# Hybrid mLSTM and dilated-attention encoder: key parts, query splits, step shares and two row loads placed differently in the second request's part

## The chip, the cores and the metric

The kernel runs on one core of a Trainium2 chip. The metric is the device time of one execution in microseconds (us). The engines are TensorE (PE, matmuls; PEld is its weight load), VectorE (DVE), ScalarE (ACT), GpSimd (POOL) and SyncE (SP, which issues DMA transfers; GpSimd issues some too).

## What is computed

One encoder layer is applied to two requests with the same weights: A (`x_prompt`, 1024 tokens) and B (`x_sample`, 512 tokens), both with 1024 channels.

```
h    = rms_norm(x, pre_w)
cols = h @ w_in                     # q|k, v, o, gates of the mLSTM; q, k, v of the attention; z's; merge gates
y_m  = mlstm_mixer(...)             # 4 heads x 256, forward and backward, chunks of 128
y_a  = dilated_attention(...)       # 3 groups x 8 heads x 64, mixed by their softmax denominators
g    = sigmoid(gate)
out  = (g0 * (y_m @ w_pm) + g1 * (y_a @ w_pa)) @ w_out
y    = x + rms_norm(out, post_w)
```

## The kernel before, in words

**Products.** All large products are float32 split in two parts of fewer bits, high and low: high times high, high times low, low times high. `mm3` (L212, L213, L214) issues these three matmuls; I call them a triple. A weight block arrives by DMA in a raw tile (`load_w`, L264, queue `self.side`), ScalarE writes its high part (L275), VectorE subtracts it for the low part (L281, `split_w`). The same split is made for queries and keys.

**Stages in time.** A's projections come first, up to about 960 us. Then `short_input` (L802) turns B's rows with TensorE transposes (L316) that ScalarE (L322) and VectorE (L323) evict into `H`; a scan of A and A's attention (1310 to 1587 us) follow; then `quad`, B's scan (about 1590 to 1782 us), B's attention (to about 2056 us), B's `combine`, and the remaining products up to the end.

**Fill.** B's projections, and later the output projections, are a list of steps, `Fill`, a step being one triple. They are woven between the instructions of the scans and attentions: `fill.stage(steps, shares)` sets a rate of steps per share, each `fill(share)` brings the count of steps up to what is due by then, and `fill.until(n)` issues what is left up to step n. `quad` asks for its stage with 192 steps (`STEPS`, L2171), of which `fill.until(SHORT)` behind it issues what has not come.

**Order.** TensorE's order is that of the code. ScalarE's, VectorE's, GpSimd's and SyncE's orders in time come from a scheduler that follows its own idea of when inputs are there; `issue_after` adds that an instruction stands behind another. So an edit in one place moves instructions of these engines elsewhere too. Each engine runs its own list strictly in order, and a DMA queue's issues are in such a list.

**quad, B's scan.** Four heads, four chunks of 128 tokens, two directions: 32 rounds. `prepare(h)` splits head h's queries (L1310 on ScalarE, L1311 on VectorE, into tile X1) and, for each chunk c, the keys: kh (L1316) and kl (L1317), one buffer each. Then two triples make the scores sc, and ScalarE evicts them (L1327, `st`). For head 0 it runs as a whole before the rounds, with a fill share of 1/5 between the chunks; for the others it begins in an earlier head's round with i = d = 1, one chunk a round. `front(k)` makes round k's weighted scores: a mask on GpSimd (L1348), an exponential on ScalarE (L1350, `rm`), products on VectorE (L1355, L1356), the high part `sch` on ScalarE (L1363) and the low part `scl` on GpSimd (L1364). `core(k)` multiplies them with the values: `num` (L1377 with sch, L1380 with scl). Its results are divided and accumulated (L1383 to L1389), normalized and, some rounds later, turned (L1407) and stored as `ym_b` (L228 from SyncE). The head's loads are `Q<-qk_b`, `V1a<-vs_b` (SyncE) and `rw<-rw_b` (GpSimd). Fill steps beside it are evicted by L755, L758, L760, L766 (o and z gates, `sw`, `sg`) and L915 (merge gates, stored as `gt_b`).

**B's attention.** `bias<-erow` is loaded by SyncE, the logits lg are made (L1675), VectorE adds the bias and finds the maximum (L1694), ScalarE exponentiates (L1698), TensorE turns the result (L1705). In A's attention the same stages of the 64-wide groups are L1574, L1585, L1589, L1597 and the output's eviction L1612. `attend` ends with `self.held = []` (L1871); until then `held` has its last evictions, behind which weight splits are put.

**combine, B.** For each of four rows: a load of the attention's output (`V0a`, `V1a<-og_b`, 792 KB, L1898) and of a gate (`az_b`, 256 KB, into `az`, `X`, `Q`), weights (L1907 to L1917), a mix (L1924) and sums (L1930) on VectorE, then a turn on TensorE (L1935). The first two rows' loads are issued together from SyncE (L1953 to L1957). Beside it run products with weight blocks `w_out` and `w_pm`, which GpSimd loads (L264). `body` calls `next(mixed)`, sets the last fill stage and issues `fill(4)` (L2409) before it goes on with the rows.

## Time and profile before

| | us |
|---|---|
| median of three runs | 2209.32 (2208.91 to 2210.37) |
| the profiled execution | 2206.59 |
| its span, first to last instruction | 2204.8 |
| TensorE busy in the span | 2185.3 |
| VectorE, ScalarE, GpSimd busy | 1463.5, 1087.3, 696.8 |
| mean granted TensorE clock | 0.998 of full speed |

How to read the profile's rows: a timeline row has start, duration, engine, line, operation and tiles, and in square brackets the idle time ahead of it and what released it. A row of the list of waits has who waited for whom, total us, times, longest. A row of the table by stretches has a stretch of the span, its length, each engine's busy time there with the number of instructions, and the clock that was granted to TensorE (1.00 is full speed). TensorE's rows overlap: a matmul of 512 columns shows some 0.39 us, while the next one starts 0.23 us after it.

### The profile page before, as it was taken

To read this page: it belongs to the slowest core of one execution; us is meant where nothing else is said; L and a number is where in the kernel's file an instruction comes from. 1 tells how busy PE (TensorE), PEld (TensorE's weight loads), DVE (VectorE), ACT (ScalarE), POOL (GpSimd) and SP (SyncE) were. 2 spreads that over 40 slices of the span, in tenths; PEclk is the share of its full clock that TensorE was granted. 3 is DMA by queue.
4 is the path that set the end of the run, shared out by engine and by line. 5 is a ranking of instruction groups with operands and counts; after the bars stand their busy time and mean duration, and the time that the engine had idled before them with its cause. 6 is when DMAs were issued, how large, how long until landed. Compare 5 with 4: busy or idle time off the path is not lost.

```text
span 2204.8 us, 34396 instructions
## 1 busy us (share of the span) xinstructions
PE 2185.3 (99%) x11962; PEld 1886.4 (86%) x11962; DVE 1463.5 (66%) x2969; ACT 1087.3 (49%) x2246; POOL 696.8 (32%) x981
## 2 busy tenths in 40 slices
PE   9999999999999999999999999999999999999998
PEld 8999888888888888888888889998788888888787
DVE  7765665657778555547888765564667855656674
ACT  7322243444444333446777656666655544544332
POOL 1000432333333222226677640011044522232221
PEclk9999999999999999999999999999999999999999
DMA  3842443423233222376746569996778786776763
GB/s 126 194 115 78 156 163 134 172 105 115 106 114 115 80 75 94 134 244 210 229 153 214 152 195 255 247 244 183 227 235 260 232 260 215 228 249 198 249 216 109
DMA packets 209144, 390.41 MB, mean 177 GB/s; under 512 B 37418, under 2 KB 123114, under 8 KB 208971
## 3 DMA queue, kind: packets, MB, share of 16 engines
q1 hardware_dynamic: 179128, 279.63, 40.5%
q0 software_dynamic: 26240, 96.00, 13.6%
q10 hardware_dynamic: 3602, 12.59, 1.4%
q8 instruction: 94, 1.54, 0.3%
q14 instruction: 80, 0.65, 0.1%
HBM read 274.70 MB, written 113.44 MB: 176 GB/s over the span
## 4 chain that ended last, share of the span: by engine, by line
PE 90%; issue 3%; DMA 2%; DVE 2%; POOL 1%; ACT 1%; SPq 0%; DVEq 0%; POOLq 0%; ACTq 0%
PE d L214 14%; PE d L212 14%; PE d L213 14%; PE dense L212 11%; PE dense L213 11%; PE dense L214 11%; PE lg L1675 2%; PE pt L1705 1%; PE o L1748 1%; PE num L212 1%; PE num L214 1%; PE num L213 1%; PE a L1095 1%; DMA wraw<-w_pm 1%; PE kv L212 1%
## 5 line engine op out<-in xcount | busy, mean ns | idle before, releaser
L212 PE MATMUL dense<-H,wh 128*128 128x512 f32 x664 | 269.5, 406 | 0.0
L213 PE MATMUL dense<-H,wh 128*128 128x512 f32 x664 | 260.6, 393 | 0.0
L214 PE MATMUL dense<-H,wl 128*128 128x512 f32 x664 | 260.6, 392 | 0.0
L213 PE MATMUL d<-Hl,phla 128*128 128x512 f32 x608 | 236.5, 389 | 0.0
L214 PE MATMUL d<-Hh,phla 128*128 128x512 f32 x608 | 236.5, 389 | 0.0
L212 PE MATMUL d<-Hh,phla 128*128 128x512 f32 x608 | 236.5, 389 | 0.0
L281 DVE TENSOR_TENSOR wl<-wraw,wh 128x1024 fp32r<-128x1024 f32 (+1 forms) x121 | 149.3, 1235 | 51.5 <-ACT wh L275 51.4
L212 PE MATMUL d<-Hh,phlb 128*128 128x512 f32 x456 | 177.4, 389 | 0.0
L213 PE MATMUL d<-Hl,phlb 128*128 128x512 f32 x456 | 177.4, 389 | 0.0
L214 PE MATMUL d<-Hh,phlb 128*128 128x512 f32 x456 | 177.4, 389 | 0.0
L275 ACT ACTIVATE wh<-wraw 128x1024 fp32r<-128x1024 f32 (+1 forms) x124 | 128.1, 1035 | 61.1 <-PE dense L213 19.5
L214 PEld LDWEIGHTS dense<-H,wl 128*128 128x128 f32 x664 | 124.8, 188 | 28.1
L696 POOL TENSOR_TENSOR psum_w<-pw_raw 128x512 f32<-128x512 f32 x38 | 55.9, 1472 | 280.9 <-DMA pw_raw<-w_in 251.2
L214 PE MATMUL d<-vhi,Hl 128*128 128x322 f32 x448 | 140.5, 314 | 0.5 <-DVE Hl L432 0.3
L212 PE MATMUL d<-vhi,Hh 128*128 128x322 f32 x448 | 140.3, 313 | 0.1
L212 PEld LDWEIGHTS dense<-H,wh 128*128 128x128 f32 x664 | 125.5, 189 | 16.8 <-issue 1.2
L213 PE MATMUL d<-vlo,Hh 128*128 128x322 f32 x448 | 139.6, 312 | 0.0
L1694 DVE CUSTOM_DVE_ANT_0 ls<-lg,bias 128x256 f32<-128x256 f32 (+2 forms) x240 | 78.8, 350 | 90.9 <-PE lg L1675 62.1
L213 PEld LDWEIGHTS dense<-H,wh 128*128 128x128 f32 x664 | 125.6, 189 | 14.9
L212 PEld LDWEIGHTS d<-Hh,phla 128*128 128x128 f32 x608 | 114.2, 188 | 23.6
L213 PEld LDWEIGHTS d<-Hl,phla 128*128 128x128 f32 x608 | 114.2, 188 | 23.6
L214 PEld LDWEIGHTS d<-Hh,phla 128*128 128x128 f32 x608 | 114.2, 188 | 23.6
(630 smaller groups left out, 5809.6 us busy)
## 6 DMA issues: line engine op xcount, KB each, us to landing
pw_raw<-w_in SPq DMA_DIRECT2D x76, 512.0 KB, 4.2
wraw<-w_in SPq DMA_DIRECT2D x63, 512.0 KB, 4.2
aqk_a<-pwk SPq DMA_DIRECT2D x40, 512.0 KB, 3.5
wraw<-w_pm POOLq DMA_DIRECT2D x24, 512.0 KB, 6.1
wraw<-w_out POOLq DMA_DIRECT2D x24, 512.0 KB, 4.1
aqk_b<-sw SPq DMA_DIRECT2D x40, 256.0 KB, 4.7
wraw<-w_v POOLq DMA_DIRECT2D x22, 430.0 KB, 6.8
qk_a<-pwk SPq DMA_DIRECT2D x16, 512.0 KB, 2.7
```

Source lines behind the costliest of these rows:

```text
L212: nc.tensor.matmul(out, lh, rh, start=start, stop=False, **kw)
L213: nc.tensor.matmul(out, lh, rl, start=False, stop=False, **kw)
L214: nc.tensor.matmul(out, ll, rh, start=False, stop=stop, **kw)
L275: high = nc.scalar.activation(hi[:, :n], raw[:, :n], AF.Copy)
L281: low = (self.lows or nc.vector).tensor_sub(lo[:, :n], raw[:, :n], hi[:, :n].bitcast(F32))
L696: self.nc.gpsimd.tensor_add(s[:, 0], ws[1][:, 0], ws[1][:, 1])
L1095: nc.tensor.matmul(p[:, c - c0], kT[:, ct, c * P:(c + 1) * P], qT[:, ct, c * P:(c + 1) * P], start=ct == 0, stop=ct == 1)
L1675: nc.tensor.matmul(lg[:, hh], q[hh][:, qs], z.rearrange("p (n j) -> p n j", j=P)[:, pair], start=z is k[hh], stop=z is not k[hh])
L1694: nc.vector.tensor_tensor_reduce(out=ls[rows, hh], in0=ts["lg"][hh][rows, of], in1=bt[rows, hh, by], scale=1.0, scalar=NEG, op0=OP.add, op ...
L1705: nc.tensor.transpose(pp[:, hh * nk + x], ts["ls"][:, hh, x * P:(x + 1) * P], self.ident)
L1748: nc.tensor.matmul(of(hh, 0, P), vh(kt[x], hh), pt[:, hh * len(kt) + x], start=x == 0, stop=x == len(kt) - 1)
```

## The change

Five edits:

1. `short_input` takes two placeholder banks of the transposes' pool with a memset, where it took one, so that the first transposes begin two banks on.
2. `attend` hands its last evictions on as `self.behind`, and the query split of the scan's head 0 is put behind these; for the other heads it is put behind the newest accumulation.
3. In `prepare`, kh has two buffers and the next chunk's high part is made before the scores of this one; kl, still with one buffer, is made after them. For heads 1 to 3 `prepare` begins a round later (i = 2, d = 0).
4. `quad` asks for 3 shares more for the same 192 steps.
5. In `combine` of B, row 1's two loads go to GpSimd's queue, behind the last weight load and behind one more `yield`; `body` issues `fill(2)`, these loads, `fill(2)`.

```diff
-        nc.vector.memset(ps.tile([P, BLK], F32, name="d")[0:1, 0:1], 0.0)
+        for _ in range(2):
+            nc.vector.memset(ps.tile([P, BLK], F32, name="d")[0:1, 0:1], 0.0)
...
-            fill.stage(steps, lead + len(rounds) + n // 4 + late)
+            fill.stage(steps, lead + len(rounds) + n // 4 + late + 3)
...
-                nc.scalar.activation(qs[0], x["q"], AF.Copy)
-                nc.vector.tensor_sub(qs[1], x["q"], qs[0].bitcast(F32))
-
-                def keys(c):
-                    k = x["k"][:, :, c * P:(c + 1) * P]
-                    kk = [sb.tile([P, 2, P], F32R, name=z, bufs=1) for z in ("kh", "kl")]
-                    nc.scalar.activation(kk[0], k, AF.Copy)
-                    nc.vector.tensor_sub(kk[1], k, kk[0].bitcast(F32))
-                    return kk
-
-                kk = keys(0)
+                of = lambda c: x["k"][:, :, c * P:(c + 1) * P]
+
+                def high(c):
+                    k = sb.tile([P, 2, P], F32R, name="kh")
+                    nc.scalar.activation(k, of(c), AF.Copy)
+                    return k
+
+                def low(c, hi):
+                    k = sb.tile([P, 2, P], F32R, name="kl", bufs=1)
+                    nc.vector.tensor_sub(k, of(c), hi.bitcast(F32))
+                    return hi, k
+
+                with ExitStack() as st_:
+                    for z in self.behind if h == 0 else self.acc[1:]:
+                        st_.enter_context(self.tc.issue_after(z.ins))
+                    nc.scalar.activation(qs[0], x["q"], AF.Copy)
+                    nc.vector.tensor_sub(qs[1], x["q"], qs[0].bitcast(F32))
+                kk = low(0, high(0))
                 yield
                 for c in range(n):
+                    coming = high(c + 1) if c < n - 1 else None
...
-                    kk = keys(c + 1) if c < n - 1 else None
+                    kk = coming is not None and low(c + 1, coming)
...
-                if i == d == 1 and h < 3:
+                if i == 2 and d == 0 and h < 3:
...
-            self.held = []
+            self.behind, self.held = self.held, []
...
-            loads(1)
+            yield
+            with self.tc.issue_after(self.loaded.ins):
+                loads(1, self.side)
...
-                fill(4)
+                fill(2)
+                next(mixed)
+                fill(2)
```

The order on the engines moves with it. First, ScalarE at the start of B's scan, from the second key of head 0 on (names: kh keys' high part, st the scores, wh a weight block's high part, sw and sg gates, sch the first product's scores). Before:

```order
L1316 ACTIVATE kh<-Q_15607 128x256
L1327 ACTIVATE st_15899<-sc 128x512
L1316 ACTIVATE kh<-Q_15607 128x256
L1327 ACTIVATE st_15899<-sc 128x512
L1350 ACTIVATE rm<-rm,col_7710 128x128
L1363 ACTIVATE sch<-rm 128x128
L1327 ACTIVATE st_15899<-sc 128x512
L1350 ACTIVATE rm<-rm,col_7710 128x128
L275 ACTIVATE wh_7698<-wraw_7696 128x1024
L755 ACTIVATE sw_7815<-dense 128x512
L1363 ACTIVATE sch<-rm 128x128
```

In the changed kernel (Q_15609 is head 0's tile, Q_16087 head 1's; L1315 stands for L1316, L1336 for L1327, L1359 for L1350, L1372 for L1363):

```order
L1315 ACTIVATE kh<-Q_15609 128x256 x3
L1336 ACTIVATE st_15901<-sc 128x512
L1315 ACTIVATE kh<-Q_15609 128x256
L1336 ACTIVATE st_15901<-sc 128x512 x3
L1315 ACTIVATE kh<-Q_16087 128x256 x2
L275 ACTIVATE wh_7698<-wraw_7696 128x1024
L755 ACTIVATE sw_7817<-dense 128x512
L1359 ACTIVATE rm<-rm,col_7710 128x128
L766 ACTIVATE sg<-sg,hnw 128x512
L1372 ACTIVATE sch<-rm 128x128
```

The first sch stood ahead of the last score's eviction and of the weight split; now it stands behind head 1's first two keys, the weight split and two gate evictions. VectorE's list has the same move: its part of rm (L1356, now L1365) stood ahead of the low part of that weight block (L281) and of L760 and now stands behind them. On TensorE the first `num` follows the last triple of that weight block directly, where a triple of the next block lay between. SyncE's loads of head 1's queries and keys stood behind a weight load that waits for this split and now stand ahead of it, behind five other loads.

Second, SyncE ahead of B's attention (gt_b stores of gates, ym_b stores of the scan's turns, bias the first tile's bias). Before:

```order
L228 DMA gt_b<-sw_7813 128x512
L228 DMA ym_b<-ym_7822 128x2x128
L228 DMA ym_a<-az_15888 128x4x128
L228 DMA gt_b<-sw_7814 128x512
L228 DMA gt_b<-sw_7815 128x512
L228 DMA ym_b<-ym_7823 128x2x128
L253 DMA bias_18083<-erow 128x256 x2
```

In the changed kernel:

```order
L228 DMA gt_b<-sw_7814 128x512
L228 DMA gt_b<-sw_7815 128x512
L228 DMA ym_b<-ym_7825 128x2x128
L264 DMA wraw_7696<-w_in 128x1024
L253 DMA bias_18083<-erow 128x256 x2
L253 DMA Q_17554<-aqk_b 64x512 x2
L253 DMA V1a<-aqk_b 64x512 x3
L253 DMA Q_17554<-aqk_b 64x512 x2
L253 DMA V1a<-aqk_b 64x512 x3
L253 DMA bias_18084<-erow 128x256 x2
L228 DMA gt_b<-sw_7816 128x512
L228 DMA gt_b<-sw_7817 128x512
```

The stores of the last two gates of this stretch (there sw_7814 and sw_7815, here sw_7816 and sw_7817, the same two tiles) stood ahead of the first bias and now stand behind the second. TensorE's list has 14 dense triples between the last turn (L1407) and the first logits (L1675), where it had none.

Third, GpSimd in B's combine (wraw a weight block's raw tile, X and V1a row 1's loads, xo the residual rows). The change's piece of the list, from the `w_out` block on:

```order
L264 DMA wraw_7697<-w_out 128x1024
L253 DMA ymr_18065<-ym_b 128x512
L264 DMA wraw_7696<-w_pm 128x1024
L253 DMA X_20643<-az_b 128x4x128
L253 DMA V1a<-og_b 128x1584
L2173 DMA xo_20634<-x_prompt 128x512
L2173 DMA xo_20635<-x_prompt 128x512
L264 DMA wraw_7697<-w_pm 128x1024
```

The fourth and fifth row stood on SyncE between `V0a<-og_b` and `Q<-az_b`; all else of this piece is as it was.

More of the change, by code (lines that the diff above doesn't have):

```diff
@@ L1895, in combine, with load @@
         az_of.at = -(T.n - 1) % len(az_of.bufs)
-        def load(t):
-            self.fetch(("og", T.S), cs[t % 2], T.og[t * P:(t + 1) * P])
+        def load(t, queue=None):
+            self.fetch(("og", T.S), cs[t % 2], T.og[t * P:(t + 1) * P], queue)
         by = lambda x: x.rearrange("p g (a b) -> p g a b", a=4)
@@ L1945, in combine, with loads @@
         az, w = {}, []
-        def loads(t):
+        def loads(t, queue=None):
             if t < T.n:
                 az[t] = az_of()
-                self.fetch(("az", T.S), az[t].rearrange("p (c s) -> p c s", c=4), T.az[:, :, t * P:(t + 1) * P].rearrange("c p s -> p c s"))
-                load(t)
+                self.fetch(("az", T.S), az[t].rearrange("p (c s) -> p c s", c=4), T.az[:, :, t * P:(t + 1) * P].rearrange("c p s -> p c s"),
+                           queue)
+                load(t, queue)
         if slow:
```

## The prediction

> **What bounds the kernel now.** I read the page's first part, then the list of TensorE's waits, then the timelines around each wait that the change touches. The page comes first:
>
> ```profile
> PE 2185.3 (99%) x11962; PEld 1886.4 (86%) x11962; DVE 1463.5 (66%) x2969; ACT 1087.3 (49%) x2246; POOL 696.8 (32%) x981
> ```
>
> TensorE is busy for 2185.3 of 2204.8 us, so 19.5 us of idle time is all that an edit which leaves its instructions alone can win, apart from its clock. The change leaves TensorE's products as they are and moves some. So the question is only which waits go, which come, and what the clock does behind them. The waits that the change touches:
>
> ```profile
> PE lg L1675 <- DVE ot L1694: 2.5, 1, 2.5
> PE dense L212 <- ACT Q L275: 1.2, 1, 1.2
> PE sc L214 <- DVE kl L1317: 0.9, 2, 0.6
> PE sc L212 <- ACT kh L1316: 0.9, 2, 0.6
> PE d L316 <- DVE d L802: 0.8, 1, 0.8
> PE dense L213 <- DVE Q L281: 0.8, 1, 0.8
> PE pt L1597 <- ACT ls L1589: 0.7, 2, 0.3
> ```
>
> The columns are total us, times, longest; the seven add up to 7.8 us. Some cost more than they show, as the table by stretches says (stretch, its length, busy time of PE, PEld, DVE, ACT and POOL with instructions in brackets, then the granted clock, DMA share, GB/s):
>
> ```profile
> 1794.40:1797.90 3.50, 3.42 (x12) 3.06 (x13) 1.09 (x8) 3.24 (x10) 0.00 (x0) 0.51 1.04 292
> 2070.90:2074.40 3.50, 3.50 (x10) 2.72 (x10) 3.02 (x6) 0.69 (x2) 2.77 (x6) 0.51 0.92 328
> ```
>
> The first stretch lies right behind the wait of 2.5 us, the second right behind the pair of 1.2 and 0.8. In both the granted clock is 0.51: 3.5 us at half speed lose 3.5 x 0.49 = 1.7 us each.
>
> **Edit 1, the second placeholder (L802).** The memset on a fresh bank waits for the last eviction of the phase before; with two placeholders the first transposes get a bank that was evicted earlier, and VectorE's late eviction is wanted only some transposes later. Gain 0.8 by the waits row, nothing at worst: **-0.8**.
>
> **Edit 2, the query split of the first head.** Here it stands in front of the softmax of attention A:
>
> ```profile
> 1565.90 1.06 ACT L1310 ACTIVATE X<-Q 128x1024 fp32r<-128x1024 f32 x1 [2.22 <-DMA Q<-qk_b]
> 1566.99 1.23 DVE L1311 TENSOR_TENSOR X<-Q,X 128x1024 fp32r<-128x1024 f32 x1 [2.51 <-ACT X L1310]
> ```
>
> ScalarE stands still 2.22 us for the load and then both engines spend 1.06 and 1.23 us, and the transposes of L1597 wait 0.7 us in all. Put behind the last evictions of A, nothing waits for it there: the first scores run at 1597.19 (below). Gain 0 to 1.1 (with what a wait costs beside its mark, see the keys), I take **-0.8**. The splits of heads 1 to 3 move behind the last accumulations of the scan and a round later, and their scores move with them; no wait of TensorE is marked for these splits now, so 0.
>
> **Edit 3, keys.** Start to start a product of 512 columns takes 0.23 us (below, 1606.28 to 1606.50). The first wait of the scan:
>
> ```profile
> 1597.19 0.40 PE L213 MATMUL sc<-X,kh 128*128 128x512 f32 x1
> 1598.19 0.50 PE L214 MATMUL sc<-X,kl 128*128 128x512 f32 x1 [0.60 <-DVE kl L1317]
> ```
>
> It stays, since the low part of key 0 still stands behind a weight split and an eviction on VectorE, and it grows: with a smaller share per step only two filler triples (0.68 us each), not three, come before the first score. **+0.7**. The other three waits (0.9 + 0.9 - 0.6 = 1.2 us) are a head's keys that a single buffer releases late; high parts made a chunk ahead and a preparation that begins a round later take these away. From the first row to the second are 1.00 us, so 0.77 is lost for 0.60 marked; by that ratio 1.2 is worth 1.5: **-1.5**, and 0 if the low part, which still has one buffer, is what comes late.
>
> **What this order costs: the first product of the scan.** ScalarE and VectorE also change their order there. Before, the split of the first scores (rm L1356, sch L1363) was done ahead of the next unit's weight split. Now sch stands behind the high part of head 1's first two keys, L275, L755 and L766, and its input rm behind L281 and L760 on VectorE; L275 itself waits for the unit's last product. And on TensorE the product that needs sch comes directly behind that unit's end, where before one triple lay between. These pieces, in time order, as they run now:
>
> ```profile
> 1606.28 0.39 PE L213 MATMUL dense<-H,wh 128*128 128x512 f32 x1
> 1606.50 0.39 PE L214 MATMUL dense<-H,wl 128*128 128x512 f32 x1
> 1607.20 1.04 ACT L275 ACTIVATE wh<-wraw 128x1024 fp32r<-128x1024 f32 x1
> 1607.32 0.29 DVE L1356 TENSOR_TENSOR rm<-rm,st 128x128 f32<-128x128 f32 x1 [2.50 <-ACT rm L1350]
> 1607.41 0.40 PE L1377 MATMUL num<-V0a,sch 128*128 128x258 f32 x2
> 1608.15 0.58 ACT L755 ACTIVATE sw<-dense 128x512 f32<-128x512 f32 x1
> 1608.27 1.23 DVE L281 TENSOR_TENSOR wl<-wraw,wh 128x1024 fp32r<-128x1024 f32 x1 [0.66 <-ACT wh L275]
> 1608.62 0.30 ACT L1363 ACTIVATE sch<-rm 128x128 fp32r<-128x128 f32 x1
> 1609.77 0.68 DVE L760 SCALAR_TENSOR_TENSOR sg<-sw,sg 128x512 f32<-128x512 f32 x1
> 1610.95 0.71 ACT L766 ACTIVATE sg<-sg,hnw 128x512 f32<-128x512 f32 x1
> ```
>
> On this clock the unit now ends one triple later: its L213 starts at 1606.96 and ends at 1607.35, and TensorE is free at 1607.41. The chain: L275 at 1607.37; L281 1.07 behind it (as 1607.20 to 1608.27) at 1608.44, over at 1609.67; L760 to 1610.3; L766 to 1611.0 (rm is ready meanwhile); sch to 1611.3. The product waits from 1607.4 to 1611.3: **3.9 us**. It is more if the keys ahead of L275 wait for head 1's load, which now goes out early, behind five transfers:
>
> ```profile
> 1591.79 4.74 DMA wraw<-w_in
> V1b<-og_a SPq DMA_DIRECT2D x1, 792.0 KB, 10.3
> Q<-qk_b SPq DMA_DIRECT2D x8, 256.0 KB, 5.2
> ```
>
> Its fourth piece is held until that weight load has landed, at 1596.5; 5.2 us later is 1601.7, 10.3 us later (the slowest transfer of this stretch) is 1606.8. Keys are needed by 1606.6 (two at 0.4 ahead of 1607.4), so 0 to 0.2 more from this, and up to 1 if it queues longer. I take **+4.1**. A wait this long can halve the clock behind it. The two stretches above say 1.7 us for each such window; it falls partly into the wait itself or takes two windows (0 to 3.4): **+1.5**.
>
> **Edit 4, the late products.** The stage's shares go up by 3: 192/38 = 5.05 steps per share becomes 192/41 = 4.68, while 38 shares are drawn, so 192 - 178 = 14 triples are left, 9.5 us of TensorE that now stand ahead of attention B's first logits. What they should cover:
>
> ```profile
> 1780.38 5.40 SPq L228 DMA_DIRECT2D gt_b<-sw  x2
> 1783.88 1.06 ACT L275 ACTIVATE Q<-wraw 128x1024 fp32r<-128x1024 f32 x1 [6.08 <-DMA wraw<-w_in]
> 1786.35 1.00 SPq L253 DMA_DIRECT2D bias<-erow  x2
> 1792.65 0.42 DVE L1694 CUSTOM_DVE_ANT_0 ls<-lg,bias 128x256 f32<-128x256 f32 x1 [5.02 <-DMA bias<-erow]
> 1793.99 0.42 DVE L1694 CUSTOM_DVE_ANT_0 ls<-lg,bias 128x256 f32<-128x256 f32 x1 [0.91 <-DMA bias<-erow]
> 1791.57 0.39 PE L214 MATMUL dense<-H,wl 128*128 128x512 f32 x1
> 1794.48 1.22 PE L1675 MATMUL lg<-V0a,Q 128*128 128x256 f32 x4 [2.52 <-DVE ot L1694]
> ```
>
> SyncE's queue sits 5.40 us on a store whose eviction stands on ScalarE behind a weight split that waits 6.08 us for its load. So the bias goes out at 1786.35, its second half lands at 1793.99, and the logits of the third tile wait: 2.91 from start to start less 0.23 are 2.7 us, and 1.7 of clock behind them. Now the last two gate stores stand behind the bias, which follows the last turn's store at once; 7.6 us (1786.35 to 1793.99) are covered by the 9.5 us of late triples alone, with two tiles' products more before the third. Both go: **-4.4**. The cover would have to be short by all of that for the gain to be 0. ScalarE has weight splits ahead of the first exponentials, whose transposes come 14 triples later too.
>
> **Edit 5, row 1's loads.** They leave SyncE for GpSimd's queue, behind two weight loads (the group rows give KB each and the median us to landing):
>
> ```profile
> V1a<-og_b SPq DMA_DIRECT2D x2, 792.0 KB, 5.4
> wraw<-w_out POOLq DMA_DIRECT2D x24, 512.0 KB, 4.1
> 2058.96 8.33 DMA wraw<-w_out
> 2066.80 0.39 PE L214 MATMUL dense<-wh,H 128*128 128x512 f32 x1
> 2068.43 0.50 PE L212 MATMUL dense<-Q,H 128*128 128x512 f32 x1 [1.24 <-ACT Q L275]
> 2069.69 0.50 PE L213 MATMUL dense<-Q,H 128*128 128x512 f32 x1 [0.76 <-DVE Q L281]
> ```
>
> The weight block took 8.33 us where the median is 4.1, and landed at 2067.29; four row loads went out around it, and the two that move are half of their bytes. TensorE loses 1.63 + 1.26 - 2 x 0.23 = 2.4 us, and 1.7 of clock. With half of the 4.2 us excess gone the block lands at 2065.2, with all of it gone at 2063.1. ScalarE's split (1.06 in the rows of L275 above) and VectorE's (1.23) then end by 2067.5 at the latest, VectorE's order having this split ahead of row 0's mixing, where before it stood behind three of those; TensorE wants it at 2067.3. At most 0.3 remains and no half clock: **-3.8**, 0 if the block is as late as before. On GpSimd's queue the residual loads stand behind the two moved ones, and they are wanted much later. Row 1's own mixing and turn come with less in hand: **+0.3**, 0 to 1.
>
> **Sum:** -0.8 - 0.8 + 0.7 - 1.5 + 4.1 + 1.5 - 4.4 - 3.8 + 0.3 = **-4.7 us**. The profiled execution took 2206.59 us, 1.8 of it outside the span, so it would take 2201.9; it lies 2.7 below the median shown, and the forecast is 2209.3 - 4.7 = **2204.6**.
>
> **A rule on the clock.** The rows above have half clock behind 2.5 us and behind 1.2 + 0.8 us of waiting, and I charge the clock to those waits. [...]
>
> **The rivals.** (a) The first product does not wait, because its chain is done sooner than I lay out: without 4.1 and 1.5 the time is 2204.6 - 5.6 = 2199.0. Against it stands the order, which puts L275 and L281 ahead of sch on both engines. (b) The change does not do what it says at attention B's start or in combine: the bias or the weight block is late again, and 4.4 or 3.8 stay, 2209.0 or 2208.4 (both, 2212.8). For it: GpSimd's queue issues more there, and a load on it shares the transfers' time with SyncE's wherever it stands. [...] (d) Slower: ScalarE's queue stands at head 1's keys. [...] For it: the transfers ahead already run at 10.3 us. Against: even that row reaches only 1606.8.
>
> **How the numbers follow.** A measurement of this kernel tells about 0.2%, 4.4 us: faster is below 2204.9, slower above 2213.7. The forecast has 0.45, of which 0.30 below 2204.9 (the halved clock, 0 to 3.4, decides that); (a) 0.20, faster; (b) 0.16, the same but for 0.01; (c) 0.08, the same; (d) 0.11, of which 0.09 slower. So faster 0.50, the same 0.40, slower 0.10. The range runs from just below (a), 2198, to between (b) and (d), 2212.
>
> **What would show it.** In the changed profile: no wait at the first transposes of B's input; one long wait num <- sch at the scan's start, with L275, L281, L760 and L766 just ahead; no sc waits but the first; half clock behind the num wait and none at attention B's start; no wait of dense for the w_out block, landing in about 5 us. I am wrong if num does not wait, if it waits much above 5 us, or if either late wait is still there.

## The result and the profile after

| | before | after |
|---|---|---|
| median, same chip and batch (7 runs each) | 2208.91 us (2206.80 to 2214.51) | 2220.49 us (2214.21 to 2222.84) |
| ratio, after to before | | 1.0047 [1.0032, 1.0062] |
| profiled execution, its span | 2206.59, 2204.8 us | 2220.49, 2218.7 us |
| mean granted clock of TensorE | 0.998 | 0.996 |

The change makes the kernel 0.5% slower, where I forecast 4.7 us less. The page of after has TensorE as busy as before; what grew is its waiting. Its busy row, then its list of waits (who waited for whom, total us, times, longest; some rows are left out):

```profile
PE 2186.4 (99%) x11962; PEld 1886.4 (85%) x11962; DVE 1460.4 (66%) x2970; ACT 1089.1 (49%) x2246; POOL 696.7 (31%) x983
```

```profile
PE num L1386 <- issue: 8.0, 1, 8.0
PE sc L213 <- DVE X L1327: 2.9, 2, 1.8
...
PE tp L1944 <- DVE cw L1918: 2.1, 1, 2.1
PE dense L212 <- DVE sw L2138: 1.5, 1, 1.5
PE lg L1684 <- DMA V1a<-aqk_a: 1.4, 1, 1.4
...
PE dense L213 <- DVE Q L281: 0.8, 1, 0.8
...
PE sc L214 <- DVE kl L1320: 0.7, 1, 0.7
```

Of the seven waits that the prediction listed in before, the bias's (2.5 us), the first transposes' (0.8) and A's last transposes' (0.7) are gone; the scan's key waits are down to the first; the pair at the `w_out` block is one of 0.8. In their place stand 8.0 us at the scan's first product, two waits for query splits, and one at row 1's turn; the rows of sw (in attention B) and aqk_a (in A's attention) come back below. The clock in three stretches (columns as in the prediction: behind the first product, behind the query split of head 3, at attention B's first logits):

```profile
1617.10:1620.60 3.50, 3.40 (x10) 2.86 (x11) 1.27 (x7) 1.30 (x6) 1.81 (x6) 0.50 0.50 197
1723.50:1727.00 3.50, 3.50 (x12) 2.79 (x11) 3.34 (x12) 3.21 (x9) 2.81 (x5) 0.54 0.64 245
1798.80:1802.30 3.50, 3.50 (x19) 2.95 (x18) 1.50 (x6) 0.60 (x1) 2.17 (x4) 1.00 1.03 216
```

So the half speed at attention B's start is cured, and two new stretches of it have come in B's scan.

**Where the time went.** The list of waits leaves out what a halved clock costs. I therefore went through TensorE's rows and summed, for each stage, by how much each start-to-start time exceeds the median for its shape in before (0.227 us for 512 columns; times below the median count as negative). I call the sum TensorE's loss. It comes from one profiled execution of each kernel, and where one stage ends and the next begins shifts a row by 0.1 to 0.3 us. Both kernels were profiled a second time, on one chip (the runs f3 and f4 below), and the last column is that second pair:

| stage | before | after | forecast | measured | second pair |
|---|---|---|---|---|---|
| A's scan, with B's first transposes (edit 1) | 5.33 | 4.32 | -0.8 | -1.01 | -1.02 |
| A's last transposes (edit 2) | 2.33 | 1.41 | -0.8 | -0.92 | -1.15 |
| first scores of B's scan | 0.93 | 1.08 | +0.7 | +0.15 | +0.18 |
| first product and clock behind it | 0.06 | 9.94 | +5.6 | +9.88 | +10.95 |
| rest of B's scan (edits 2, 3) | 3.87 | 8.27 | -1.5 | +4.40 | +5.42 |
| first 25 us of attention B (edit 4) | 4.47 | 0.10 | -4.4 | -4.37 | -6.30 |
| rest of attention B | 5.37 | 7.38 | 0 | +2.01 | -1.19 |
| `w_out` block (edit 5) | 4.16 | 1.15 | -3.8 | -3.01 | -2.00 |
| rows' turns behind it (edit 5) | 0.13 | 2.42 | +0.3 | +2.29 | +4.21 |
| A's projections | 7.10 | 6.49 | 0 | -0.61 | +0.53 |
| A's attention | 9.43 | 15.06 | 0 | +5.63 | +0.03 |
| sum (a last stage of -0.07 left out) | 43.18 | 57.62 | -4.7 | +14.44 | +9.66 |

The executions differ by 2220.49 - 2206.59 = 13.90 us, and in the second pair by 2218.66 - 2209.52 = 9.14 us, so the sums account for nearly all of it. The ratio of the medians is worth 0.0047 x 2209 = 10.4 us. A's attention is no part of the change (f3 below): without it the first pair gives 8.8 us and the second 9.6. The +2.01 in the rest of attention B is the wait of 1.5 us for sw in the list above and one of 0.8 for H; the second profile of after has no such wait for sw, and the stage loses less than before there.

**The first product.** The timeline of after, in time order, from SyncE's issue of head 1's queries and keys to the first `num` (the row marked SPq is the issue of the four pieces), then the group row of that load (KB each, median us from issue to landing):

```profile
1598.90 2.58 SPq L253 DMA_DIRECT2D Q<-qk_b  x4
1608.86 0.39 PE L214 MATMUL dense<-H,wl 128*128 128x512 f32 x1
1612.62 0.72 ACT L1315 ACTIVATE kh<-Q 128x256 fp32r<-128x256 f32 x2 [4.78 <-DMA Q<-qk_b]
1613.25 1.04 ACT L275 ACTIVATE wh<-wraw 128x1024 fp32r<-128x1024 f32 x1
1614.33 1.23 DVE L281 TENSOR_TENSOR wl<-wraw,wh 128x1024 fp32r<-128x1024 f32 x1 [0.83 <-ACT wh L275]
...
1616.18 0.72 ACT L766 ACTIVATE sg<-sg,hnw 128x512 f32<-128x512 f32 x1 [1.12 <-DVE sg L760]
1616.81 0.29 ACT L1372 ACTIVATE sch<-rm 128x128 fp32r<-128x128 f32 x1
1617.20 0.77 PE L1386 MATMUL num<-V0a,sch 128*128 128x258 f32 x2 [7.96 <-issue]
```

```profile
Q<-qk_b SPq DMA_DIRECT2D x4, 256.0 KB, 11.7
```

Read it from the end. `num` waits for sch, the last of these rows on ScalarE, and the chain from L275 to sch is the one I laid out: 1613.25 to 1617.10. But ScalarE does not start L275 when TensorE has finished the unit (at 1609.25). It stands 4.78 us at head 1's first keys. Their load was issued between 1598.90 and 1601.48; its last piece, issued at 1601.16, landed at 1612.52, and ScalarE went on at 1612.62. The wait is some 4 us of load (ScalarE could have begun L275 at 1609.25 and began at 1613.25) and 4 us of chain.

**The query split of head 3.** Rows of VectorE, ScalarE and TensorE in after:

```profile
1719.01 1.05 ACT L1326 ACTIVATE X<-Q 128x1024 fp32r<-128x1024 f32 x1
1720.23 0.74 DVE L1364 SCALAR_TENSOR_TENSOR rm<-st,cols,rw 128x128 f32<-128x128 f32 x2 [0.31 <-POOL scl L1373]
1720.89 0.34 DVE L1364 SCALAR_TENSOR_TENSOR rm<-st,col,rw 128x128 f32<-128x128 f32 x1
1721.15 1.21 DVE L1327 TENSOR_TENSOR X<-Q,X 128x1024 fp32r<-128x1024 f32 x1
1722.42 0.50 PE L213 MATMUL sc<-X,kh 128*128 128x512 f32 x1 [1.80 <-DVE X L1327]
```

ScalarE's half of the split stands behind the newest accumulation and runs at 1719.01. VectorE's half is ready to run at 1720.06. Its list has three products of a later round's weighted scores (L1364) first, which wait 0.31 us for GpSimd. So the half runs from 1721.15 to 1722.36; TensorE could have used it some 0.23 us after its product of 1720.11. The clock behind this wait is the 0.54 of the second stretch above.

### The profile page after: what moved, and what is told of

The parts are those of the page before. It is cut to its first block, busy times and chain, and to the rows that moved or that the text cites. A ratio compares the mean times of both kernels' runs of the same rounds, so it can differ in the third digit from the quotient of the medians.

```text
span 2218.7 us, 34381 instructions
## 1 busy us (share of the span) xinstructions
PE 2186.4 (99%) x11962; PEld 1886.4 (85%) x11962; DVE 1460.4 (66%) x2970; ACT 1089.1 (49%) x2246; POOL 696.7 (31%) x983
## 4 chain that ended last, share of the span: by engine, by line
PE 89%; DMA 5%; issue 2%; DVE 2%; ACT 1%; POOL 0%; SPq 0%; DVEq 0%; POOLq 0%; ACTq 0%
PE d L214 14%; PE d L212 14%; PE d L213 14%; PE dense L212 11%; PE dense L213 11%; PE dense L214 11%; PE lg L1684 2%; PE pt L1714 1%; PE num L212 1%; PE num L214 1%; PE num L213 1%; PE num L1386 1%; DMA sraw<-ym_a 1%; PE o L1757 1%; DMA wraw<-w_pm 1%
## 5 line engine op out<-in xcount | busy, mean ns | idle before, releaser
L281 DVE TENSOR_TENSOR wl<-wraw,wh 128x1024 fp32r<-128x1024 f32 (+1 forms) x121 | 149.4, 1236 | 56.6 <-ACT wh L275 56.5
L275 ACT ACTIVATE wh<-wraw 128x1024 fp32r<-128x1024 f32 (+1 forms) x124 | 128.3, 1036 | 65.7 <-PE dense L213 26.1
```

The lines of the kernel that those rows point to most:

```text
L275: high = nc.scalar.activation(hi[:, :n], raw[:, :n], AF.Copy)
L281: low = (self.lows or nc.vector).tensor_sub(lo[:, :n], raw[:, :n], hi[:, :n].bitcast(F32))
```

## The experiments

Each is told by its edit against the kernel named; TensorE's loss is reckoned as in the table, and the ratio is to the kernel before on the same chip in the same batch.

**e1_keys_late: the first keys of heads 1 to 3 behind the newest scores.** Against after:

```diff
-                kk = low(0, high(0))
+                with ExitStack() as st_:
+                    if h > 0:
+                        st_.enter_context(self.tc.issue_after(self.weighted.ins))
+                    kk = low(0, high(0))
...
-                nc.scalar.activation(hi, rm, AF.Copy)
+                self.weighted = nc.scalar.activation(hi, rm, AF.Copy)
```

> The change with one order added: the first keys of heads 1 to 3 (high and low part) are put behind the newest high part of the weighted scores, so head 1's load no longer stands ahead of the first product's scores on ScalarE. Theory (the first product waits for two things in turn, head 1's load at 5 us and the chain behind the unit's end at 3.9 us): the wait of num falls from 8.0 to 3.9 to 4.5 us, the half clock behind it stays, time 4 us less than the changed kernel, some 2216. Rival (the load alone made it, the rest of the chain would fit under TensorE's work): the wait falls to under 1 us and the time by 8 to 9.5. Rival (the loss lies in the late products or in the row loads): no change beyond 2 us.

Measured: 2211.38 us, ratio 1.0002 [0.9994, 1.0011]. In its list of waits and on ScalarE's timeline:

```profile
PE num L1389 <- issue: 3.8, 1, 3.8
```

```profile
1611.49 1.06 ACT L275 ACTIVATE wh<-wraw 128x1024 fp32r<-128x1024 f32 x1 [1.22 <-PE dense L213]
```

With the keys behind sch, L275 waits for TensorE alone, and the wait at `num` is 3.8 us, the 3.9 of the prediction's chain. So 8.0 - 3.8 = 4.2 us of after's wait were the load. The time fell by more than the 4 us expected (some 10 us by the two ratios), because the new order also moved the query splits (2.9 to 1.1 us marked, the rest of the scan 8.27 to 3.61).

**e2_split0: query splits of heads 1 to 3 without the accumulation ahead.** Against after:

```diff
-                    for z in self.behind if h == 0 else self.acc[1:]:
+                    for z in self.behind if h == 0 else ():
```

> The change, but the query splits of heads 1 to 3 are not put behind the newest accumulation; head 0's still is put behind the last evictions of A's attention. Theory (these splits come too late in heads 2 and 3, and sc L213 waits 2.9 us for VectorE's part, with half clock behind the second): the waits of sc for X go, and 3 to 5 us with them; the first product's wait grows by about 1 us, since head 1's split now stands on ScalarE ahead of its scores behind the same load. In all 2 to 4 us less than the changed kernel. Rival (these splits are late because the preparation begins a round later): the waits stay and the time does not move by more than 1 us.

Measured: 2217.71 us, ratio 1.0032 [1.0020, 1.0044]. No wait for X is left at the scores, the rest of the scan loses 3.01 us where after loses 8.27, and the price is at the first product, where head 1's query split now stands ahead of sch too:

```profile
PE num L1386 <- issue: 8.8, 1, 8.8
```

So the place of the query splits behind the accumulation costs 8.27 - 3.01 = 5.3 us in the scan, and the rival, that the later start of the preparation makes them late, is out: it starts as late here.

**e3_shares_back: the three shares taken back.** Against after:

```diff
-            fill.stage(steps, lead + len(rounds) + n // 4 + late + 3)
+            fill.stage(steps, lead + len(rounds) + n // 4 + late)
```

> The change without the 3 shares more, so that the whole stage of 192 steps is drawn in the scan and no triples are left for the gap ahead of B's attention. Theory (the shares moved the unit's end to just before the first product, and with it ScalarE's order): the wait of num falls from 8.0 to some 1.2 us (weight split 1.0, gate eviction 0.5 and sch 0.3 behind the unit's end, less one triple), its half clock of 1.4 goes, and the wait for the bias ahead of the third logits comes back with 2.7 and 1.7: some 4 us less than the changed kernel. Rival (the late products gained nothing): no wait for the bias either, 8 us less. Rival (shares do not bear on the first product): num still waits 8 and the time rises by 4.

Measured: 2214.46 us, ratio 1.0015 [1.0004, 1.0026].

```profile
PE lg L1684 <- DVE ot L1703: 3.0, 1, 3.0
...
PE num L1386 <- issue: 1.0, 1, 1.0
```

With the old shares the first `num` waits 1.0 us and the bias is late again (the first 25 us of attention B lose 6.10 us). By the two ratios the time is 7 us below after's, for 4 expected; the query splits stay late (4.0 us of waits for X).

**e4_comb_back: row 1's loads on SyncE again.** Against after:

```diff
-            yield
-            with self.tc.issue_after(self.loaded.ins):
-                loads(1, self.side)
+            loads(1)
...
-                fill(2)
-                next(mixed)
-                fill(2)
+                fill(4)
```

> The change with row 1's loads of the combine back on SyncE's queue and the four steps of filling in one piece. Theory (edit 5 gave about 3 us at the weight block and lost 2.3 at row 1's turn): the wait of dense for the block of w_out comes back to 2.0 us with half clock behind it, the wait of tp for cw L1918 goes; the time is within 1.5 us of the changed kernel. Rival (the moved loads are where the loss lies, by their sharing of the transfers' time): 3 us less or more than that. Rival (edit 5 is as good as forecast, 3.8 us): 3 us or more above the changed kernel.

Measured: 2217.56 us, ratio 1.0025 [1.0015, 1.0034].

```profile
PE dense L213 <- DVE Q L281: 1.0, 1, 1.0
PE dense L212 <- ACT Q L275: 0.8, 1, 0.8
PE tp L1944 <- DVE cw L1918: 0.7, 1, 0.7
```

The waits for the `w_out` block are back, and row 1's turn does not wait; the 0.7 us are at row 2's. The block's stage loses 2.36 us, not the 4.16 of before's profile: much the same waits as there, without half clock behind them (products of 512 columns start 0.23 us apart from 2067.36 on). The two stages together lose 3.4 us here, 3.6 in after and 5.1 in its second profile. By the ratios the time is nearer the rival's than the theory's, 0.0022 or 4.9 us below after; the two come from different batches and their intervals overlap, so this is not shown.

**e5_free: also the weight split and its unit's gate evictions behind the first sch.** Against e1_keys_late (in `quad`, from `front(0)` to round 1; `held` is what weight splits stand behind, `th` the eviction of L755):

```diff
+            self.first = self.held = [self.weighted]
...
+                if k == 1:
+                    self.first = self.held = []
...
-        nc.scalar.activation(th, c, AF.Tanh, scale=0.5)
+        with ExitStack() as st:
+            for x in getattr(self, "first", ()):
+                st.enter_context(self.tc.issue_after(x.ins))
+            nc.scalar.activation(th, c, AF.Tanh, scale=0.5)
```

> The change with the order of the scan's start set right: the first keys of heads 1 to 3 behind the newest weighted scores (as in the run with the keys put late), and also the next weight split and the gate units' first evictions behind the first product's scores until the second product is out. Theory (the wait of num was head 1's load plus this chain): num's wait is under 0.5 us and no half clock follows, 5 us less than the run with the keys late. Rival (the scores' own inputs are late too, the mask's row or the last st): 1 to 3 us of wait remain.

Measured: 2206.90 us, ratio 0.9992 [0.9980, 1.0003]. The stage of the first product loses 0.94 us (5.48 in e1, 9.94 in after). The one wait left for a sch is 0.6 us, at the second product (its row is that of e6 below). Against e1 the stage is 4.5 us better, near the 5 expected; by the ratios the time fell by 0.0010, which is 2.2 us.

**e6_free2: and the query splits behind the newest scores.** Against e5_free:

```diff
-                    for z in self.behind if h == 0 else self.acc[1:]:
+                    for z in self.behind if h == 0 else [self.weighted]:
```

> As the run before, and the query splits of heads 1 to 3 stand behind the newest weighted scores' high part and not behind the newest accumulation. Theory (the accumulation is late on VectorE, the scores' high part is not): sc L213's waits for X, 1 to 3 us in all in the change, fall below 1 us, and the time is 0.5 to 2 us less than the run before. Rival (the splits are late because ScalarE and VectorE are busy there, whatever they are put behind): no difference beyond 0.5 us.

Measured: 2207.07 us, ratio 0.9988 [0.9979, 0.9998]. Its list of waits has no X and no long num:

```profile
PE tp L1953 <- DVE cw L1927: 2.9, 1, 2.9
...
PE num L1392 <- ACT sch L1378: 0.6, 1, 0.6
```

The rest of the scan loses 3.03 us, and e5's waits for X (1.6 us) are gone, as the theory has it; the time does not tell e6 from e5. With all five edits in place and only the order of ScalarE's and VectorE's lists mended, the kernel is just faster than before.

**e7_only_shares: before with edit 4's three shares alone** (the diff of e3 the other way round, on before).

> The kernel before with the 3 shares more alone (late products), nothing else of the change. Theory (the shares alone move the unit's end before the first product, and the scheduler then puts head 1's keys and its query split ahead of the first scores): num waits 8 us or more, half clock behind it, and the bias wait with its half clock (4.4) is gone: 4 to 7 us slower than before. Rival (the order came from the early high parts or the placed query splits): num waits under 1 us and the time is 4 us less than before.

Measured: 2210.72 us, ratio 1.0007 [0.9996, 1.0018].

```profile
PE num L1376 <- issue: 6.7, 1, 6.7
```

```profile
1607.60 0.42 ACT L1313 ACTIVATE kh<-Q 128x256 fp32r<-128x256 f32 x1 [4.17 <-DMA Q<-qk_b]
...
1608.40 1.05 ACT L1317 ACTIVATE X<-Q 128x1024 fp32r<-128x1024 f32 x1
1609.34 1.05 ACT L275 ACTIVATE wh<-wraw 128x1024 fp32r<-128x1024 f32 x1
```

The shares alone bring the long wait, with the bias cured (0.10 us lost at attention B's start). The time is not 4 to 7 us above before's, as expected, but level with it; the stage of the first product loses 8.9 us and the rest of the scan only 1.8. Head 1's first key and query split stand ahead of L275 on ScalarE here, and ScalarE stands 4.17 us for their load. Together with e3 this shows that edit 4, not the edits on keys and splits, turned the order of ScalarE's list.

**e8_only_memset: before with edit 1 alone.**

```diff
-        nc.vector.memset(ps.tile([P, BLK], F32, name="d")[0:1, 0:1], 0.0)
+        for _ in range(2):
+            nc.vector.memset(ps.tile([P, BLK], F32, name="d")[0:1, 0:1], 0.0)
```

> The kernel before with the second placeholder alone. Theory: the first transposes do not wait (0.8 to 0.9 us), all else as before: within 0.2% of before, some 1 us less, and the waits of A's attention for its loads (lg for aqk_a, 0.7 to 4.8 us in the changed kernel's and the other runs' profiles, none in the profile of before) show up here too or not by chance. Rival (starting the scan 1 us earlier brings these load waits): they show up with 1 us or more and the time is not below before.

Measured: 2210.75 us, ratio 1.0002 [0.9992, 1.0012]. The first transposes do not wait (A's scan stage 4.31 us, before 5.33), and the bias is late as in before. The timing cannot tell one us from nothing. The rest of the scan loses 3.1 us, without edits 2 and 3. A's attention loses 12.35 us, with logits that wait 1.0, 0.8 and 0.3 us for loads.

**f1_free2_noloads: e6_free2 with edit 5 undone** (its diff is that of e4).

> The order of e6_free2 (edits 1 to 4 with head 1's keys, the weight split, the gate evictions and the query splits placed behind the newest scores), with edit 5 undone: row 1's loads on SyncE again. Theory that edit 5 gains at the w_out block and pays at row 1's turn: the w_out waits come back (TensorE's loss in that stage from about 0 to 2.4 to 4.2 us) and the wait at the turn falls from 4.7 to about 1 us, so the time is about that of e6_free2, ratio to before 0.9975 to 0.9995. Rival, that the loads are worth the 3.8 us I forecast: ratio about 1.0005, slower than e6_free2 by 0.0017.

Measured: 2206.43 us, ratio 0.9967 [0.9953, 0.9980]. Its waits, and the stretch behind the `w_out` block:

```profile
PE tp L1953 <- DVE cw L1927: 2.2, 1, 2.2
PE dense L213 <- DVE Q L281: 1.2, 1, 1.2
...
PE dense L212 <- ACT Q L275: 0.6, 1, 0.6
```

```profile
2067.50:2071.00 3.50, 3.50 (x9) 2.68 (x9) 3.38 (x6) 0.69 (x3) 3.43 (x7) 0.53 0.95 272
```

The block's waits are back as expected, here with half clock (3.98 us lost). But the wait at row 1's turn stays at 2.2 us with the loads on SyncE, so the moved loads are not its only cause (below). Its ratio is the lowest of all, below the expected range, and the rival's 1.0005 lies outside its interval: nothing here speaks for 3.8 us by edit 5. Its median is within 0.7 us of those of e5 and e6; the median of before was 2212.88 us in this batch and 2209.19 in theirs, and I do not rank the three.

**f2_only_loads: before with edit 5 alone.**

> The kernel before with edit 5 alone. Theory: the w_out waits lose 3 to 4 us of TensorE, row 1's turn waits 1 to 3 us, 0 to 2 us gained: ratio 0.999 to 1.000. Rival, that the moved loads gain their 3.5 us net as forecast: ratio 0.9984.

Measured: 2210.94 us, ratio 0.9992 [0.9980, 1.0004]: the interval holds both theories. In its profile the `w_out` block loses 0.09 us and the turns 3.18, together 3.3; in before's two profiles they lose 4.3 and 2.9. So by TensorE's loss edit 5 is worth something between 1.0 us gained and 0.4 lost.

The stretch right behind its wait at the turn, which is 2.9 us long:

```profile
2098.80:2102.30 3.50, 3.50 (x18) 2.96 (x19) 3.11 (x9) 1.02 (x2) 0.08 (x1) 1.00 1.06 393
```

**f3_before_again: before, unchanged.**

> The kernel before, unchanged, profiled once more. Theory that the loss in A's attention (9.4 us in its profile, 10.0 to 16.9 in all later ones) depends on when its loads happen to land and not on the change: this profile shows 10 to 15 us there, with the logits waiting for aqk_a loads. Rival, that the change causes it: 9 to 10 us again and no such waits.

Measured: one run, 2209.52 us. A's attention loses 11.55 us, with logits waiting for loads (0.8 and 0.3 us), none of which before's first profile had. The stretch right behind its `w_out` waits (0.4 and 1.4 us here):

```profile
2073.10:2076.60 3.50, 3.50 (x16) 2.89 (x17) 3.50 (x6) 1.03 (x3) 3.30 (x7) 1.00 0.96 300
```

The clock is whole, where before's first profile has 0.51.

**f4_after_again: after, unchanged.**

> The changed kernel, unchanged, profiled once more. Theory: the wait at the first product of the scan (8.0 us), at the query splits of heads 2 and 3 (1.3 and 2.1 us with half clock) and at row 1's turn (2.3 us) are there again, each within 1 us; A's attention loses anything from 9 to 17 us. Rival, that they come by chance: one of them is gone.

Measured: one run, 2218.66 us. All three waits are there again, A's attention loses 11.58 us:

```profile
PE num L1386 <- issue: 9.0, 1, 9.0
PE sc L213 <- DVE X L1327: 2.8, 2, 1.8
PE tp L1944 <- DVE cw L1918: 2.7, 1, 2.7
```

```profile
2107.00:2110.50 3.50, 3.50 (x12) 2.87 (x13) 3.10 (x9) 1.04 (x2) 0.10 (x1) 0.61 1.06 405
```

The stretch lies behind the turn, at 0.61 of the clock.

## Why the prediction was wrong, step by step

Three terms of the sum failed, the first two by their mechanism. Head 1's load was priced at 0 to 0.2 us and cost 4.2 at the first product. The query splits of heads 1 to 3 were put at 0 and cost 5.3 in the scan. Edit 5 was put at -3.8 + 0.3 = -3.5, and its two stages gave -0.7 us in the first pair and +2.2 in the second. The first pair has another 5.6 us in A's attention that are no part of the change.

**Edit 1, right.** -0.8 forecast, -1.0 measured, and again in e8 alone.

**Edit 2, right for head 0, wrong for the others.** Head 0's part gave -0.92 for -0.8. For heads 1 to 3 I wrote "no wait of TensorE is marked for these splits now, so 0". That step failed: an operation for which nobody waits may still be just in time, and it was moved behind another operation without a look at what its engine's list has ahead of it there. In e2 the move is undone for these heads and the rest of the scan loses 3.01 us instead of 8.27.

**Edit 3, not shown.** The first key's wait grew by 0.15, not 0.7. In after the key waits behind the first are gone, as forecast, but the row "rest of B's scan" holds the query splits too. With those mended (e2, e6) the stage is 3.01 and 3.03, 0.9 us below before, for 1.5 forecast. Kernels without edit 3 reach as much: 3.1 us in e8, 3.2 in f2 and 1.8 in e7, which has no key wait behind the first either. So these waits move with any change of the order, and no run here isolates what edit 3 gains.

**The first product: chain right, load wrong.** The chain of 3.9 us came as worked out (e1: 3.8). The load failed: "Keys are needed by 1606.6 [...] so 0 to 0.2 more from this". I counted 10.3 us from 1596.5, the landing of the weight block that holds its fourth piece. After's scan starts 1.5 us later than before's (first scores at 1598.48, there 1596.95), so 1.5 us come off its times here. The fourth piece was held by that block, as I wrote: the block landed at 1601.14 and the piece was issued at 1601.16. But that is 1599.7 on the prediction's clock, 3.2 us later than I had it, because the block itself was issued later (at 1594.0, in before at 1591.79). The piece then took 11.4 us, and ScalarE got its keys at 1612.62 - 1.5 = 1611.1, 4.5 us after they were needed. Nor was 10.3 us the slowest transfer of before's stretch. Before's trace has a gate load there, issued directly behind the one of 10.3 us, that took 12.2; the group row hides it, since it shows the median of two (4.1 and 12.2):

```profile
X<-G_b SPq DMA_DIRECT2D x2, 256.0 KB, 8.2
```

Rival (d) named the place, ScalarE standing at head 1's keys, and that part happened; I gave it 0.11. From after to e1, without the 4.2 us of load, the stage loses 9.94 - 5.48 = 4.5 us less, about one us of TensorE per us of load. At that rate a landing at 1611.1 gives 2204.6 + 4.5 = 2209.1 us, so it does not account for the measured time alone. The halved clock behind the wait was there, as forecast (1.5 forecast, 9.94 - 8.0 = 1.9 measured; the clock is 0.50 from 1614.07 to 1620.90, and 3.1 us of that lie inside the wait).

**Edit 4, right in place and size, but the cost at the first product is its too.** The bias wait and its clock went, -4.37 for -4.4. The order shown ahead of the prediction was already the scheduler's answer to these shares; e7 and e3 show by addition and by removal that the shares alone put head 1's keys ahead of sch. Alone they bring the wait of 6.7 us and come out level with before: by TensorE's loss edit 4 loses 8.9 us at the first product and wins 4.4 at attention B and 2.1 in the rest of the scan.

**Edit 5, mis-sized on both sides.** The block is earlier: issued at 2073.25, it let ScalarE go at 2080.21, 7.0 us for 8.33, and one wait of 0.8 is left. The rows of after:

```profile
2073.25 0.54 POOL L264 DMA_DIRECT2D wraw<-w_out  x1 [8.95 <-DVE wl L281]
2080.21 1.06 ACT L275 ACTIVATE Q<-wraw 128x1024 fp32r<-128x1024 f32 x1 [2.08 <-DMA wraw<-w_out]
...
2092.76 0.18 DVE L1918 TENSOR_TENSOR cw<-V1a,cw 128x24 f32<-128x24 f32 x1
2094.66 1.23 DVE L281 TENSOR_TENSOR wl<-wraw,wh 128x1024 fp32r<-128x1024 f32 x1 [1.72 <-ACT wh L275]
...
2097.43 1.23 DVE L281 TENSOR_TENSOR wl<-wraw,wh 128x1024 fp32r<-128x1024 f32 x1 [0.27 <-ACT wh L275]
2098.57 0.20 DVE L1926 SCALAR_TENSOR_TENSOR cw<-cw,wd 128x24 f32<-128x24 f32 x1
```

Of the 3.8 us forecast, 1.7 were the half clock behind the block's waits in the one execution that I had read. Without edit 5 the same stage loses 4.16 us in before's first profile and 3.98 in f1, both with half clock, and 2.4 to 2.6 without it in before's second profile, e4, e7 and e8. So the half clock was there in two of six. Against the price, row 1's turn, I put 0.3. It is 2.3, and 4.2 in the second pair, where half clock joins. VectorE has two weight splits between L1918 and L1926 of row 1, 5.8 us from one to the other, where before needs 1.3 (its L1909 runs at 2081.34, its L1917 at 2082.67). From there to the row's last sum, for which the turn waits, it is 17.5 us in after and 8.2 in before. (The list of waits names L1918 because row 2's stands directly behind that sum.) The 14 profiles divide by this order: in nine the two splits stand between, and row 1's turn waits 1.7 to 2.9 us in each; in the other five, e4 and e7 among them, they do not, and it does not wait. Edit 5 alone brings this order (f2), but so does the mended order of the scan without edit 5 (f1). So the order of VectorE's list explains the wait, and more than one edit leads to that order; the place of the loads is not needed for it.

**A's attention, nothing of the change.** The second profile of before loses 11.55 us there and the second of after 11.58, so the 5.6 us of the first pair are chance. All profiles lie between 9.4 and 16.9 us. What differs is the logits' waits for loads (none in before's first profile, 3.1 us in after's) and the clock: the five profiles with a stretch of half clock there (after, 0.50 from 1381.96 to 1385.38, and e1, e2, e4, e5) lose 13.6 us or more, the other nine 12.7 or less. Why the landings differ is left open. My base, an execution of 2206.59 us, was among the best: I corrected for the median, not for the fact that its stages were lucky.

**The clock.** Half clock stands behind 8.0 us at the first product (0.50) and behind 1.80 us at head 3's split (0.54). Behind the turn of row 1 it is 1.00 in f2 (2.9 us) and 0.61 in f4 (2.7 us); behind the `w_out` pair 0.51 in before (2.0 us), 1.00 in f3 (1.8 us), 0.53 in f1 (1.8 us). So waits of 2 to 3 us sometimes halve the clock and sometimes do not, in the same place.

The traces show when it changed. In all 14 the granted clock changes only at whole multiples of 3.413 us after its first change. In before it changes first at 12.69, then, up to TensorE's last products, at 1794.44, 1797.86, 2070.92 and 2074.34, which are 522, 523, 603 and 604 steps on; in after first at 9.81, then at 1381.96, 1385.38, 1614.07, 1620.90, 1723.30 and 1726.71, which are 402, 403, 470, 472, 502 and 503. For each such step I took the share in which TensorE is idle, by the busy times of the profile. It is 0.73 and 0.49 in the steps that end at before's 1794.44 and 2070.92, where half clock begins, and 0.55, 1.00 and 0.56 in those that end at after's 1381.96, 1614.07 and 1723.30. The 14 traces have some 8900 steps at full clock. Of these, the 22 with an idle share of 0.55 or more are all followed by half clock, and of those up to 0.44 none is; of the seven between, from 0.45 to 0.53, three are. A wait that lies inside one step is whole in that step's share, and one that a boundary cuts is split over two. The two steps that share f2's wait, and the one that holds f4's:

```profile
2093.60:2097.02 3.42, 2.25 (x10) 1.51 (x9) 3.42 (x5) 0.65 (x1) 1.10 (x2) 1.00 0.85 280
2097.02:2100.43 3.41, 1.66 (x10) 1.47 (x11) 3.01 (x10) 0.22 (x1) 0.56 (x1) 1.00 1.05 402
2104.35:2107.76 3.41, 0.77 (x6) 0.76 (x7) 3.04 (x9) 0.22 (x1) 1.09 (x2) 1.00 1.02 399
```

TensorE is idle for 0.34 and 0.51 of f2's steps, with full clock behind them (1.00 above), and for 0.77 of f4's, with half clock behind it. In the same way before's `w_out` pair lies in one step (idle 0.49, 0.50 of the clock behind it), and f3's in two (0.32 and 0.21, 1.00 behind them). An estimate from these shares, for this kernel: one wait below 0.45 x 3.41 = 1.5 us would not halve the clock, one above 2 x 0.53 x 3.41 = 3.6 us would, and between them it would depend on where it falls. A term of 1.7 us per wait of 2 to 3 us should therefore have been 0 or 1.7. That the stretches behind edits 4 and 5 stay, (c) with its 0.08, did not occur: they went with their waits (in after the clock is 1.00 from 1798.80 to 1802.30 and from 2081.50 to 2088.50), and half clock stands behind a wait of 1.80 us at head 3's split.

**Rival (a), (b).** (a) did not occur in after; e5 and e6 reach it by another order (0.94 us lost in the stage of the first product), and with it the kernel is at 0.9992 and 0.9988. (b) did not occur: the bias is not late, and the weight block's stage loses 1.2 us where it lost 4.2.

## What to carry to other kernels

Where a small change of a rate makes a scheduler redraw an in-order list, look for instructions that wait for a load ahead of a chain that TensorE needs, and price the load by when it will be issued and by what single transfers at its place took, not by the median of a group. An operation without a marked wait is not free to move: ask how late it may come and what the engine's list has ahead of it at the new place. Read a stage from more than one profiled execution before you price what it would gain; in before's first the `w_out` stage had 1.7 us of half clock that its second lacked.

## What was unexpected of the hardware

A 256 KB load that lands in 5.2 us in the median of before's stretch took 11.7 us when four of them were issued behind others (a median of four, after). The granted clock behind like waits of TensorE, 1.8 to 2.9 us, was 0.51 to 0.61 in some executions and 1.00 in others: 1.00 where the wait was split over two of the steps of 3.413 us (idle shares 0.34 and 0.51 in f2, 0.32 and 0.21 in f3), halved where it lay in one (0.49 in before, 0.77 in f4). Counted from the span's start, the steps begin at 12.69 us in before and at 9.81 in after.
